# Feed-forward of a two-part float32 product: activations' hi and lo parts side by side as 512 moving columns

## The chip, the cores and the metric

The kernel runs on one core of one Trainium2 chip. The metric is device time in microseconds (us) of one execution; the median of three runs is given. TensorE (PE) multiplies matrices, with its weight loads shown apart (PEld), VectorE is called DVE, ScalarE ACT, GpSimd POOL, SyncE SP. The kernel's matmul results go to eight banks of PSUM, each of 128 partitions by 512 float32 numbers; everything else lies in SBUF.

## What is computed

256 tokens of 1024 numbers go through eight feed-forward stages and four mixers, in float32, one after another:

```python
def _swiglu(h, w_gate, w_up, w_down):
    return (jax.nn.silu(h @ w_gate) * (h @ w_up)) @ w_down

# first block, twice: feed-forward, mixer (rwkv, then mla), feed-forward, each behind an rms norm
x = x + 0.5 * _swiglu(_rmsnorm(x, g[0]), w_gate, w_up, w_down)
...
# second block, twice: feed-forward, mixer (nsa, then hgrn), feed-forward, each followed by a layer norm
x = _layer_norm(alpha * x + 0.5 * _swiglu_2(x, w_gate, w_up, w_down), gain, bias)
```

`w_gate` and `w_up` are 1024 x 2816, `w_down` is 2816 x 1024, and each stage has its own. The stages are FFN1, rwkv, FFN2, FFN3, mla, FFN4, FFN5, nsa, FFN6, FFN7, hgrn, FFN8. Only the feed-forward stages are changed.

## The kernel before

Float32 accuracy is had by two parts: a number is hi + lo, each in PE's float32r format, and a product is taken as ah bh + ah bl + al bh, three matmuls. `mm3` (L169 to L181) issues them: for each 128 rows of the contraction the two products with the stationary hi part, then those with the stationary lo part.

`weights` (L155) loads 1 MB of a weight matrix by a DMA of SP's queue (L165) into one of four staging tiles (`st0`, `st1`, and the stage's own `xst0`, `xst1`), and `hi_lo` (L149) splits it, half by half: ACT copies to hi (L152: `sp0h`, `sp1h`, `xsp0h`, `xsp1h`), DVE subtracts for lo (L153: `sp0l` and so on). There are four split tiles, too, used in turn.

The activations stand transposed, as `xTh` and `xTl`, each 128 x 8 x 256 (`new_xT`, L190; `transpose_split`, L196, writes them out of a bank, ACT the hi part, DVE the lo part).

A feed-forward stage (`_ffn`, L334) goes over the 2816 hidden channels in 11 units of 256. In the usual unit the weights are stationary and the 256 tokens stream. Its four blocks of 128 channels are gate 0, gate 1, up 0 and up 1; a block has a bank of its own and takes 24 matmuls of 256 columns. Behind them come, for each half of the channels, Silu on ACT (L346, `s`), the product with up on DVE (L351, `h`), its hi part by ACT (L402, `hTh`) and its lo part by DVE (L403, `hTl`). Then PE does the down product of the unit before: 24 matmuls in which 512 columns of the down weights stream, into four banks `acc` that collect over the whole stage. Four banks `rot` go round for everything else.

All stages but FFN1 start while the stage before is still finishing the second half of the tokens (`self.second`, called by `finish`). There the first two units go token block by token block: 128 tokens are stationary, and 256 columns of the weights stream. Their results `h` are transposed later (`late`). At a stage's end the last unit's down product has no work behind it: units 9 and 10 are multiplied token block by token block, and what follows on ACT and DVE is the split of the next stage's first weights.

A scheduler orders each engine's instructions by its own estimates; a queue's order is then fixed, and each engine works in order.

## Time and profile before

| what | value |
| --- | --- |
| three runs | 2179.0 to 2186.6 us, median 2181.73 us |
| profiled execution, span | 2183.2 us |
| PE busy | 2128.8 us, 98% |
| PE weight loads busy | 1955.2 us, 90% |
| DVE busy | 1253.8 us, 57% |
| ACT busy | 1003.9 us, 46% |
| eight feed-forward stages | about 190 us each (FFN2 390 to 580) |

Shares are of the span. Matmuls are pipelined: the duration that a row gives for one is longer than the distance from its start to the next one's, and it is that distance that counts. A row "x8" is eight instructions alike, and its time is that of all together. The profiled execution is one of its own, beside the three runs.

### The profile page before, as it was taken

Reading aid. Unit: us, or ns where it says so; the run is one execution under the profiler, and the core shown is the slowest. Engines: PE = TensorE matmul, PEld = TensorE weight load, DVE = VectorE, ACT = ScalarE, POOL = GpSimd, SP = SyncE. Lnnn points to the kernel's source line nnn. Section 1 sums busy time; section 2 is a strip of 40 time slices with the busy share of each in tenths; the row PEclk is TensorE's granted clock in tenths of the full one; section 3 lists DMA queues with packets and bytes.
Section 4 is the critical chain, followed back from the end, with each engine's and each line's share of the span. In section 5 each row is a group of like instructions: output and inputs, shape, how many; then the busy total and the mean of one; then the engine's idle time right before and its main releaser. Section 6 shows DMA issues by size and latency. Waiting matters only on the chain. (4 is left out here: it accounts for less than half of the span.)

```text
span 2183.2 us, 36275 instructions
## 1 busy us (share of the span) xinstructions
PE 2128.8 (98%) x15049; PEld 1955.2 (90%) x15049; DVE 1253.8 (57%) x2034; ACT 1003.9 (46%) x1750; POOL 183.8 (8%) x344
## 2 busy tenths in 40 slices
PE   8999999999999999999998999999999999999998
PEld 7998887999999977999897998689999999988997
DVE  5554765645555467645553566765565546766554
ACT  5444643544444455544442445544434444444442
POOL 2001050000100032000000010100000000241000
PEclk9999999999999999999999999999999999999999
DMA  9653433555556344755468563165546546326551
GB/s 302 207 180 99 141 104 119 203 187 180 176 196 205 121 135 150 239 175 192 145 212 171 168 205 116 39 205 182 192 155 225 187 155 199 130 78 232 187 185 54
DMA packets 271349, 367.63 MB, mean 168 GB/s; under 512 B 6865, under 2 KB 236853, under 8 KB 271184
## 3 DMA queue, kind: packets, MB, share of 16 engines
q1 hardware_dynamic: 263984, 348.48, 48.2%
q0 software_dynamic: 5088, 15.79, 3.3%
q8 instruction: 118, 1.93, 0.4%
q10 hardware_dynamic: 2112, 1.05, 0.2%
q14 instruction: 47, 0.39, 0.1%
HBM read 358.87 MB, written 6.42 MB: 167 GB/s over the span
## 5 line engine op out<-in xcount | busy, mean ns | idle before, releaser
L181 PE MATMUL rot<-xTh,sp0h 128*128 128x256 f32 (+1 forms) x976 | 243.3, 286 | 0.8 <-ACT xTh L205 0.8
L181 PE MATMUL rot<-xTl,sp0h 128*128 128x256 f32 (+1 forms) x976 | 240.3, 283 | 0.7 <-DVE xTl L206 0.7
L181 PE MATMUL rot<-xTh,sp1h 128*128 128x256 f32 x960 | 240.5, 287 | 0.0
L181 PE MATMUL rot<-xTl,sp1h 128*128 128x256 f32 x960 | 237.1, 283 | 0.0
L153 DVE TENSOR_TENSOR sp0l<-st,sp0h 128x1024 fp32r<-128x1024 f32 (+4 forms) x126 | 144.4, 1163 | 86.0 <-ACT sp0h L152 85.9
L181 PEld LDWEIGHTS rot<-xTh,sp0h 128*128 128x128 f32 (+1 forms) x976 | 186.7, 192 | 5.0 <-ACT xTh L205 1.7
L181 PEld LDWEIGHTS rot<-xTl,sp0h 128*128 128x128 f32 (+1 forms) x976 | 186.8, 192 | 2.7 <-DVE xTl L206 1.3
L181 PEld LDWEIGHTS rot<-xTh,sp1h 128*128 128x128 f32 x960 | 184.0, 192 | 3.1 <-issue 2.0
L181 PEld LDWEIGHTS rot<-xTl,sp1h 128*128 128x128 f32 x960 | 184.3, 192 | 0.7
L153 DVE TENSOR_TENSOR xsp0l<-xst,xsp0h 128x1024 fp32r<-128x1024 f32 (+4 forms) x106 | 116.8, 1128 | 103.8 <-ACT xsp0h L152 103.7
L351 DVE TENSOR_TENSOR h<-rot,s 128x256 f32<-128x256 f32 x176 | 74.3, 422 | 158.3 <-PE rot L181 147.1
L152 ACT ACTIVATE sp0h<-st 128x1024 fp32r<-128x1024 f32 (+4 forms) x126 | 122.0, 1003 | 83.2 <-issue 33.7
L153 DVE TENSOR_TENSOR xsp1l<-st,xsp1h 128x1024 fp32r<-128x1024 f32 x80 | 95.6, 1221 | 98.3 <-ACT xsp1h L152 98.3
L152 ACT ACTIVATE xsp0h<-xst 128x1024 fp32r<-128x1024 f32 (+4 forms) x106 | 99.5, 979 | 106.2 <-DMA xst<-in_ffn_w_gate_dram 65.4
L153 DVE TENSOR_TENSOR sp1l<-st,sp1h 128x1024 fp32r<-128x1024 f32 (+3 forms) x108 | 122.4, 1146 | 35.7 <-ACT sp1h L152 35.5
L181 PE MATMUL rot<-xTh,sp0l 128*128 128x256 f32 (+1 forms) x976 | 141.8, 282 | 0.0
L181 PE MATMUL rot<-xTh,sp1l 128*128 128x256 f32 x960 | 140.2, 283 | 0.0
L153 DVE TENSOR_TENSOR sp1l<-xst,sp1h 128x1024 fp32r<-128x1024 f32 x80 | 95.6, 1220 | 73.1 <-ACT sp1h L152 73.1
L152 ACT ACTIVATE xsp1h<-st 128x1024 fp32r<-128x1024 f32 x80 | 81.1, 1052 | 109.7 <-PE rot L181 39.8
L181 PEld LDWEIGHTS rot<-xTh,sp0l 128*128 128x128 f32 (+1 forms) x976 | 127.4, 191 | 0.2 <-issue 0.2
L181 PEld LDWEIGHTS rot<-xTh,sp1l 128*128 128x128 f32 x960 | 126.2, 192 | 0.0
L346 ACT ACTIVATE s<-rot 128x256 f32<-128x256 f32 x176 | 66.2, 376 | 130.1 <-PE rot L181 109.9
(573 smaller groups left out, 5360.4 us busy)
## 6 DMA issues: line engine op xcount, KB each, us to landing
st<-in_ffn_w_up_dram SPq DMA_DIRECT2D x47, 1024.0 KB, 5.3
st<-in_ffn_w_gate_dram SPq DMA_DIRECT2D x47, 1024.0 KB, 5.2
xst<-in_ffn_w_down_dram SPq DMA_DIRECT2D x47, 1024.0 KB, 5.1
xst<-in_ffn_w_up_dram SPq DMA_DIRECT2D x41, 1024.0 KB, 5.3
st<-in_ffn_w_down_dram SPq DMA_DIRECT2D x41, 1024.0 KB, 4.9
xst<-in_ffn_w_gate_dram SPq DMA_DIRECT2D x40, 1024.0 KB, 5.3
st<-in_even_w_in_dram SPq DMA_DIRECT2D x12, 1024.0 KB, 5.2
st<-in_hgrn_w_in_dram SPq DMA_DIRECT2D x8, 1024.0 KB, 5.6
```

The source lines that it names most:

```text
L152: self.nc.scalar.activation(hi[:, s], src[:, s], AF.Copy)
L153: self.nc.vector.tensor_sub(lo[:, s], src[:, s], hi[:, s].bitcast(F32))
L181: self.last_mm = nc.tensor.matmul(out, a, b, start=start and i == 0, stop=stop and i == n - 1).ins
L346: self.last_act = nc.scalar.activation(s, g, AF.Silu).ins
L351: self.last_mul = nc.vector.tensor_mul(h, u, s).ins
```

## The change

`xTh` and `xTl` become the two halves of one tile `xT`, 128 x 8 x 2 x 256, so that for each of the eight k blocks the 256 hi columns and the 256 lo columns stand side by side. In the usual unit, `mm_wide` replaces `mm3`: a stationary hi block of the weights is multiplied by all 512 columns at once, hi results in the lower half of the bank, lo results in the upper; the stationary lo block by the 256 hi columns, into the lower half. A block has 8 matmuls of 512 columns and 8 of 256. The halves are then added by `joined`: ACT copies the upper half to SBUF (`g`), DVE adds the lower to it. Silu and product take `g`.

The first two units become one of 512 channels: weights come as four k blocks by 512 columns, two loads for gate and two for up, and 512 columns of weights stream through the tokens, 24 matmuls of 512 per matrix and token block; Silu and product are 512 wide.

The core of the diff (the rest takes comments out):

```diff
     def new_xT(self, pool=None):
         pool = pool or self.keep
-        hi = pool.tile([P, KD, T], F32R, tag="xTh", name=self.n("xTh"))
-        lo = pool.tile([P, KD, T], F32R, tag="xTl", name=self.n("xTl"))
-        return hi, lo
+        both = pool.tile([P, KD, 2, T], F32R, tag="xT", name=self.n("xT"))
+        return both[:, :, 0, :], both[:, :, 1, :], both
+
+    def mm_wide(self, b, terms):
+        nc, n = self.nc, len(terms)
+        for i, (wh, _, _, both) in enumerate(terms):
+            nc.tensor.matmul(b, wh, both.rearrange("p a n -> p (a n)"), start=i == 0, stop=False, skip_group_check=True)
+        for i, (_, wl, xh, _) in enumerate(terms):
+            self.last_mm = nc.tensor.matmul(b[:, :T], wl, xh, start=False, stop=i == n - 1, skip_group_check=True).ins
...
+        def joined(b):
+            g = self.ff.tile([P, T], F32, tag="g", name=self.n("g"))
+            nc.scalar.activation(g, b[:, T:], AF.Copy)
+            nc.vector.tensor_add(g, b[:, :T], g)
+            return g
...
-            ws = [(unit(wg, u), unit(wu, u)) for u in range(2)]
+            ws = [[self.weights(w, k0, 4, 0, 2 * N) for k0 in (0, 4)] for w in (wg, wu)]
             for t in range(2):
...
-                for u in range(2):
-                    b = []
-                    for wh, wl in ws[u]:
-                        b.append(self.bank())
-                        self.mm3(b[-1][:, :N], [(xT[0][:, k, ts], xT[1][:, k, ts], wh[:, k, :], wl[:, k, :])
-                                                for k in range(KD)], True, True)
-                    if t and u == 0:
+                b = []
+                for halves in ws:
+                    b.append(self.bank())
+                    for j, (wh, wl) in enumerate(halves):
+                        self.mm3(b[-1], [(xT[0][:, 4 * j + k, ts], xT[1][:, 4 * j + k, ts], wh[:, k, :], wl[:, k, :])
+                                         for k in range(4)], j == 0, j == 1)
+                    if t and len(b) == 1:
...
-                    h = mul(act(b[0][:, :N]), b[1][:, :N])
-                    late.append((h, ys[u], t, 0, 2))
+                h = mul(act(b[0], 2 * N), b[1], 2 * N)
+                late += [(h[:, u * N:(u + 1) * N], ys[u], t, 0, 2) for u in range(2)]
...
-                    self.mm3(b[-1][:, :T], [(wh[:, k, s], wl[:, k, s], xT[0][:, k, :], xT[1][:, k, :])
-                                            for k in range(KD)], True, True)
+                    self.mm_wide(b[-1], [(wh[:, k, s], wl[:, k, s], xT[0][:, k, :], xT[2][:, k])
+                                         for k in range(KD)])
...
-                h = mul(act(b[i][:, :T]), b[2 + i][:, :T])
+                h = mul(act(joined(b[i])), joined(b[2 + i]))
```

The lines of `_ffn` get other numbers: in the changed kernel the copy is L365, the add L366, Silu L354, the product L359, hTh L417, hTl L418, `mm_wide` L200 and L202, the layer norm's last step L291, `transpose_split` L209 to L214.

The order on PE in the last unit of FFN2, the end of block gate 0 and the start of gate 1, before (`rot` are the banks, `xTh` and `xTl` the moving activations, `sp0h` and `sp0l` the gate weights):

```order
L181 MATMUL rot_5772<-xTh_4099,sp0h_5766 128x256
L181 MATMUL rot_5772<-xTl_4100,sp0h_5766 128x256
L181 MATMUL rot_5772<-xTh_4099,sp0l_5767 128x256 x8
L181 MATMUL rot_5797<-xTh_4099,sp0h_5766 128x256
L181 MATMUL rot_5797<-xTl_4100,sp0h_5766 128x256
```

The first three blocks of the same unit in the changed kernel (`sp0` gate, `sp1` up):

```order
L200 MATMUL rot_5280<-xT_3876,sp0h_5274 128x512 x8
L202 MATMUL rot_5280<-xT_3876,sp0l_5275 128x256 x8
L200 MATMUL rot_5297<-xT_3876,sp0h_5274 128x512 x8
L202 MATMUL rot_5297<-xT_3876,sp0l_5275 128x256 x8
L200 MATMUL rot_5322<-xT_3876,sp1h_5316 128x512 x8
L202 MATMUL rot_5322<-xT_3876,sp1l_5317 128x256 x8
```

Sixteen matmuls of 256 columns for the hi part, alternating, have become eight of 512; the eight for the lo part stand as before.

DVE behind the same unit, at the end of FFN2, before; `rot_5830` and `rot_5855` are the two up blocks, `sp0l` and `sp1l` the next stage's first weights:

```order
L351 TENSOR_TENSOR h_5884<-rot_5830,s_5882 128x256
L153 TENSOR_TENSOR sp0l_6008<-st_830_6005,sp0h_6007 128x1024
L403 TENSOR_TENSOR hTl_5881<-h_5884,hTh_5880 128x256
L153 TENSOR_TENSOR sp0l_6008<-st_830_6005,sp0h_6007 128x1024
L351 TENSOR_TENSOR h_5890<-rot_5855,s_5888 128x256
L153 TENSOR_TENSOR sp1l_6016<-st_833_6013,sp1h_6015 128x1024
L403 TENSOR_TENSOR hTl_5881<-h_5890,hTh_5880 128x256
L153 TENSOR_TENSOR sp1l_6016<-st_833_6013,sp1h_6015 128x1024
```

The same place in the changed kernel (`rot_5339` is the last up block, `g_5375` its sum):

```order
L359 TENSOR_TENSOR h_5366<-g_5363,s_5361 128x256
L153 TENSOR_TENSOR sp0l_5495<-st_897_5492,sp0h_5494 128x1024
L418 TENSOR_TENSOR hTl_5357<-h_5366,hTh_5356 128x256
L153 TENSOR_TENSOR sp0l_5495<-st_897_5492,sp0h_5494 128x1024
L366 TENSOR_TENSOR g_5375<-rot_5339,g_5375 128x256
L153 TENSOR_TENSOR sp1l_5503<-st_900_5500,sp1h_5502 128x1024
L359 TENSOR_TENSOR h_5378<-g_5375,s_5373 128x256
L153 TENSOR_TENSOR sp1l_5503<-st_900_5500,sp1h_5502 128x1024
L418 TENSOR_TENSOR hTl_5357<-h_5378,hTh_5356 128x256
```

The add of the last up block stands behind the split of the first weights, and one half of the next split stands between it and the product. On ACT the same place reads, before:

```order
L346 ACTIVATE s_5882<-rot_5772 128x256
L346 ACTIVATE s_5888<-rot_5797 128x256
L152 ACTIVATE sp0h_6007<-st_830_6005 128x1024
L402 ACTIVATE hTh_5880<-h_5884 128x256
L152 ACTIVATE sp0h_6007<-st_830_6005 128x1024
L152 ACTIVATE sp1h_6015<-st_833_6013 128x1024 x2
L402 ACTIVATE hTh_5880<-h_5890 128x256
```

and in the changed kernel:

```order
L365 ACTIVATE g_5358<-rot_5280 128x256
L354 ACTIVATE s_5361<-g_5358 128x256
L365 ACTIVATE g_5363<-rot_5322 128x256
L365 ACTIVATE g_5370<-rot_5297 128x256
L152 ACTIVATE sp0h_5494<-st_897_5492 128x1024
L354 ACTIVATE s_5373<-g_5370 128x256
L417 ACTIVATE hTh_5356<-h_5366 128x256
L152 ACTIVATE sp0h_5494<-st_897_5492 128x1024
L365 ACTIVATE g_5375<-rot_5339 128x256
L152 ACTIVATE sp1h_5502<-st_900_5500 128x1024 x2
L417 ACTIVATE hTh_5356<-h_5378 128x256
```

Four copies are added; the copy of the last up block stands behind both halves of the first split, and two halves of the second stand between it and the last `hTh`.

PE in the tail of FFN2, in the changed kernel, from the second half of unit 9's down product on (`hTh_5214` is unit 9's, `hTh_5356` unit 10's, `acc_3908` and `acc_3909` the first token block's banks, `acc_3910` the second's):

```order
L181 MATMUL acc_3909<-xsp0h_5384,hTh_5214 128x512
L181 MATMUL acc_3909<-xsp0l_5385,hTh_5214 128x512
L181 MATMUL acc_3909<-xsp0h_5384,hTl_5215 128x512 x2
L181 MATMUL acc_3908<-xsp1h_5392,hTh_5356 128x512
L181 MATMUL acc_3908<-xsp1l_5393,hTh_5356 128x512
L181 MATMUL acc_3909<-xsp1h_5392,hTh_5356 128x512
L181 MATMUL acc_3909<-xsp1l_5393,hTh_5356 128x512
L181 MATMUL acc_3910<-xsp0h_5384,hTh_5214 128x512
L181 MATMUL acc_3910<-xsp0l_5385,hTh_5214 128x512
L181 MATMUL acc_3908<-xsp1h_5392,hTh_5356 128x512
L181 MATMUL acc_3908<-xsp1l_5393,hTh_5356 128x512
L181 MATMUL acc_3908<-xsp1h_5392,hTl_5357 128x512
```

Before, the six matmuls of a bank stood together; now those that take the first half of unit 10's channels come first for both banks, then two of the second token block, and the second half of the channels behind them.

DVE at the start of FFN7, where the layer norm of the second token block (`x_82`) meets the split of the third weights, before:

```order
L278 BN_AGGR mv_16415<-bn_16412 128x2
L282 SCALAR_TENSOR_TENSOR x_82<-x_82,mv_16415,gain_16221 128x512 x2
L283 SCALAR_TENSOR_TENSOR x_82<-x_82,mv_16415,gain_16223 128x512 x2
L153 TENSOR_TENSOR xsp0l_16288<-xst_2202_16285,xsp0h_16287 128x1024 x2
L351 TENSOR_TENSOR h_16353<-rot_16326,s_16351 128x256
L153 TENSOR_TENSOR xsp1l_16296<-xst_2205_16293,xsp1h_16295 128x1024 x2
```

and in the changed kernel:

```order
L286 BN_AGGR mv_14688<-bn_14685 128x2
L290 SCALAR_TENSOR_TENSOR x_82<-x_82,mv_14688,gain_14549 128x512 x2
L291 SCALAR_TENSOR_TENSOR x_82<-x_82,mv_14688,gain_14551 128x512
L153 TENSOR_TENSOR xsp0l_14615<-xst_2373_14612,xsp0h_14614 128x1024 x2
L291 SCALAR_TENSOR_TENSOR x_82<-x_82,mv_14688,gain_14551 128x512
L214 TENSOR_TENSOR xT_14553<-rot_14696,xT_14553 128x4x128
L153 TENSOR_TENSOR xsp1l_14623<-xst_2376_14620,xsp1h_14622 128x1024 x2
L214 TENSOR_TENSOR xT_14553<-rot_14703,xT_14553 128x4x128
```

The split of the third weights (`xsp0l`) now stands ahead of the layer norm's last operation.

## Rows read from the trace of the kernel before

**Rows 1.** the page: span; busy time, share, instructions

```profile
span 2183.2 us, 36275 instructions
...
PE 2128.8 (98%) x15049; PEld 1955.2 (90%) x15049; DVE 1253.8 (57%) x2034; ACT 1003.9 (46%) x1750; POOL 183.8 (8%) x344
```

**Rows 2.** windows: length, busy (instructions) of PE PEld DVE ACT POOL, clock, DMA, GB/s

```profile
438.95:450.46 11.51, 11.51 (x97) 11.50 (x96) 5.57 (x6) 5.79 (x8) 0.00 (x0) 1.00 0.64 223
450.46:455.93 5.47, 5.47 (x26) 4.53 (x25) 3.03 (x4) 1.61 (x3) 0.00 (x0) 1.00 0.39 130
```

**Rows 3.** windows: the next whole unit, columns as in rows 2

```profile
455.93:472.91 16.98, 16.98 (x121) 16.02 (x120) 8.60 (x10) 7.17 (x10) 0.00 (x0) 1.00 0.57 183
```

**Rows 4.** windows: a unit of the seventh stage, columns as in rows 2

```profile
1743.29:1748.92 5.63, 5.63 (x27) 4.53 (x26) 3.03 (x4) 1.56 (x3) 0.00 (x0) 1.00 0.57 182
1748.92:1760.30 11.38, 11.38 (x97) 11.38 (x96) 5.58 (x6) 5.79 (x8) 0.00 (x0) 1.00 0.62 211
```

**Rows 5.** windows of PE alone: a first-unit token block, fourth and seventh stage

```profile
875.56:887.28 11.72, 11.72 (x96) 1.00 0.72 229
1631.98:1645.12 13.14, 12.36 (x99) 1.00 0.78 206
```

**Rows 6.** timeline, seventh stage: start, us, instruction, [idle before, releaser]

```profile
1636.28 1.42 DVE L283 SCALAR_TENSOR_TENSOR x<-x,mv,gain 128x512 f32<-128x512 f32 x2 [0.44 <-POOL mv L228]
1637.61 2.35 DVE L153 TENSOR_TENSOR xsp0l<-xst,xsp0h 128x1024 fp32r<-128x1024 f32 x2
...
1638.88 0.39 PE L181 MATMUL rot<-xsp0l,xTh 128*128 128x256 f32 x1 [0.78 <-DVE xsp0l L153]
```

**Rows 7.** source line L1618: durations ns min/median/max, starts

```profile
L1618 ACT ACTIVATE V<-rot x8: 383/384/387, 1826.6 to 1849.4; 128x256 f32<-128x256 f32 x8
```

**Rows 8.** lines by form: count | busy us, mean ns | idle, releasers

```profile
L153 DVE TENSOR_TENSOR sp0l<-st,sp0h 128x1024 fp32r<-128x1024 f32 x110 | 132.5, 1221 | 72.2 <-ACT sp0h L152 72.1
...
L152 ACT ACTIVATE sp0h<-st 128x1024 fp32r<-128x1024 f32 x110 | 112.1, 1052 | 77.7 <-issue 33.7 <-PE rot L181 17.7 <-PE acc L181 9.8
...
L351 DVE TENSOR_TENSOR h<-rot,s 128x256 f32<-128x256 f32 x176 | 74.3, 422 | 158.3 <-PE rot L181 147.1 <-PE rot L201 10.6
```

**Rows 9.** timeline, second stage: a weight split and its first use

```profile
496.54 2.35 DVE L153 TENSOR_TENSOR xsp1l<-st,xsp1h 128x1024 fp32r<-128x1024 f32 x2
...
506.88 0.28 PE L181 MATMUL rot<-xTh,xsp1h 128*128 128x256 f32 x1
```

**Rows 10.** timeline, end of the second stage

```profile
566.54 1.06 ACT L152 ACTIVATE sp0h<-st 128x1024 fp32r<-128x1024 f32 x1 [2.32 <-DMA st<-in_ffn_w_gate_dram]
...
569.33 0.40 PE L181 MATMUL acc<-xsp0h,hTh 128*128 128x512 f32 x1
...
570.70 0.42 ACT L402 ACTIVATE hTh<-h 128x256 fp32r<-128x256 f32 x1
...
572.53 0.39 PE L181 MATMUL acc<-xsp1h,hTh 128*128 128x512 f32 x1
```

**Rows 11.** DMA issues: KB each, us to landing

```profile
sk<-bs POOLq DMA_DIRECT2D x1, 3072.0 KB, 35.2
```

**Rows 12.** timeline, fifth stage, ACT

```profile
1192.05 1.06 ACT L152 ACTIVATE xsp0h<-xst 128x1024 fp32r<-128x1024 f32 x1 [27.23 <-DMA xst<-in_ffn_w_gate_dram]
```

**Rows 13.** waits of PE: us in total, times, longest

```profile
PE rot L181 <- ACT xsp1h L152: 10.0, 2, 9.3
```

**Rows 14.** timeline, first stage, PE

```profile
15.00 0.41 PE L181 MATMUL rot<-xTl,sp0h 128*128 128x256 f32 x1
15.21 0.41 PE L181 MATMUL rot<-xTh,sp0h 128*128 128x256 f32 x1
```

More of the change, by code (lines that the diff above doesn't have):

```diff
@@ L342, in hT, with act, mul @@
             return yh, yl
-        def act(g):
-            s = self.ff.tile([P, N], F32, tag="s", name=self.n("s"))
+        def act(g, n=N):
+            s = self.ff.tile([P, n], F32, tag="s", name=self.n("s"))
             self.last_act = nc.scalar.activation(s, g, AF.Silu).ins
             return s
-        def mul(s, u):
-            h = self.ff.tile([P, N], F32, tag="h", name=self.n("h"))
+        def mul(s, u, n=N):
+            h = self.ff.tile([P, n], F32, tag="h", name=self.n("h"))
             self.last_mul = nc.vector.tensor_mul(h, u, s).ins
             return h
+        def joined(b):
[3 more added lines that the diff above has]
+            return g
         ys, todo, first, late = [], [], 0, []
@@ L363, in _ffn @@
                     self.finish()
-                for u in range(2):
-                    b = []
-                    for wh, wl in ws[u]:
-                        b.append(self.bank())
-                        self.mm3(b[-1][:, :N], [(xT[0][:, k, ts], xT[1][:, k, ts], wh[:, k, :], wl[:, k, :])
-                                                for k in range(KD)], True, True)
-                    if t and u == 0:
+                b = []
[5 more added lines that the diff above has]
+                    if t and len(b) == 1:
                         while late:
                             self.transpose_split(*late.pop(0))
-                    h = mul(act(b[0][:, :N]), b[1][:, :N])
-                    late.append((h, ys[u], t, 0, 2))
-                todo = [(0, ys[0]), (1, ys[1])]
+                h = mul(act(b[0], 2 * N), b[1], 2 * N)
+                late += [(h[:, u * N:(u + 1) * N], ys[u], t, 0, 2) for u in range(2)]
+            todo = [(0, ys[0]), (1, ys[1])]
         NU = F // N
```

## The prediction

> **What bounds the kernel now.** I read the page first. The span is 2183.2 us and TensorE (PE) is busy in 98% of it [rows 1], so only what shortens PE's own stream, or what lets PE stand still, moves the end. Then I cut one steady feed-forward unit of the second stage (390 to 580 us) into its two parts by the windows view. The 96 matmuls of 256 columns take 11.51 us, the 24 of 512 columns 5.47 us, with PE busy throughout and the granted clock at 1.00 (its 2.4 GHz level) [rows 2]. That is 11.51 / 96 = 119.9 ns for a matmul of 256 columns and 5.47 / 24 = 227.9 ns for one of 512. Two of the small ones take 239.8 ns, one of the large ones 227.9: joining a pair is worth 11.9 ns where PE is never waiting. In the next whole unit of 16.98 us VectorE (DVE) is busy 8.60 us and ScalarE (ACT) 7.17 us [rows 3]: both have half their time free. Last I looked at the places where PE does wait: the starts of stages, their tails, and one stall.
>
> **Units behind the first ones.** A block (gate or up, 128 hidden channels) is now 8 matmuls of 512 and 8 of 256 in place of 24 of 256: 8 pairs joined, 32 in a unit, 0.38 us of 16.98. The first stage has 11 such units, the other seven 9 each: 74 units, 2368 pairs, 2368 x 11.9 ns = 28.2 us. How far can the price of a pair be off? The row of rows 2 is one unit. In a unit of the seventh stage, whose weights lie in other buffers, the 24 wide ones take 5.63 us (234.6 ns each) and the 96 small ones 11.38 us (118.5 ns) [rows 4]. With 234.6 against 119.9 a pair is worth 5.2 ns, with both prices of that unit 2.4 ns. The wide matmul that the change adds streams activations through stationary weights, where the timed wide one streams weights through stationary activations; no row shows that form. I take 11.9, since the first price is that of nearly all units and the form of the stationary part is the same 128x128, and keep 2.4 as the lower end.
>
> A rule of the Trainium skill speaks against most of this gain: "TensorE: Matmul & The Clock Gate", section "Back-to-back issue gap", gives an isolated matmul N / 2.4 ns and some 2.5 ns more, so that joining two saves 2.5 ns; 3040 pairs would then give 7.6 us. The rows above disagree with it for the steady units: 119.9 ns is 13.2 over 256 / 2.4 = 106.7.
>
> **First two units.** Per token block 96 matmuls of 256 become 48 of 512: 48 pairs, two token blocks, seven stages, 672 pairs, 8.0 us at 11.9 ns. One such block without a stall took 11.72 us for 96 matmuls, 122.1 ns each [rows 5]; at that price a pair is worth 16.3 ns and the sum 11.0. I take 8.0 and keep 11.0 as the upper end. The weights are the same bytes in pieces of 512 columns.
>
> In the seventh stage this part takes 13.14 us with PE busy for 12.36 [rows 5]: 0.78 us of idle lie in it. DVE does the last two layer-norm operations (1.42 us) ahead of the split of the third weights, and the split begins only at 1637.61, where PE needs it; PE's wait ends at 1638.88 [rows 6]. In the new order one of the two operations stands behind that split (the order of DVE above), so it can start 0.7 us sooner. The eighth stage has the same wait. I count 0.5 us for each, 1.0 (bounds 0 and 1.6).
>
> **What is added.** Per block one ACT copy of 256 columns out of a bank and one DVE add: 296 of each. An ACT copy of this form stands elsewhere in the trace at 384 ns [rows 7]; for the add I take the product of the same size, 422 ns [rows 8]. A unit gains 4 x 0.384 = 1.5 us on ACT (7.17 to 8.7) and 4 x 0.422 = 1.7 us on DVE (8.60 to 10.3), both below the new unit of 16.6 us. I cost them at nothing in the steady units. What hides them: a bank comes round again after three other blocks (2.8 us each) and a down product (5.5 us), 13.8 us, against a copy, an add and at most two splits of weights ahead of each; the weights that the splits make ready are done at 498.9, and PE takes them up at 506.88 [rows 9], 8 us of slack; the hidden channels are consumed a unit later. If that cover were gone, a unit would wait at least once for a copy and an add, 0.81 us, twice the 0.38 that it gains; nothing in the rows is that near.
>
> **Tails.** At the end of a stage the cover is short: the last unit's channels are consumed at once. In the second stage the last block ends and the down product begins at 569.33. ACT writes the last hTh from 570.70 on, done at 571.12, and PE takes it up at 572.53, 14 matmuls later: 1.4 us of slack [rows 10]. Now the chain behind the last block E is longer. One after the other come the ACT copy (0.38), the DVE add (0.42), half a weight split that stands next on DVE (1.22, [rows 8]), the product (0.42), and hTh on ACT (0.42), whose own queue has two halves of a split (2.1) in the meantime: 2.9 us. I allow 0.3 for the passes from engine to engine, and 0.5 to 1.2 for the half split that DVE is in when the copy is done: E + 3.7 to E + 4.4. In the new order of PE 18 matmuls stand ahead of the first use of that half (12 of unit 9, four with the other half of the channels, two of the next token block): 18 x 228 ns, E + 4.1. The lo part has another half split ahead of it and is due three matmuls later, so it is late by a little more. Each tail loses between nothing and 2 us (a whole split more ahead of the copy). I take 0.4, near the late end, in seven tails (behind the eighth stage no weights are split): -2.8 us.
>
> **Stall.** In the fifth stage a transfer of 3 MB that takes 35.2 us [rows 11] holds up the weights: ACT waits 27.23 us for a gate matrix, until 1192.05 [rows 12], and PE 9.3 us for a split of weights [rows 13]. The transfer is issued behind a unit's last activation, so it moves with the work, but what PE saves while it runs is waited for again: two units of 16.98 us, -0.8 us.
>
> **Cold clock.** At the start of the first stage, at the 1.2 GHz level, small matmuls follow one another in 0.21 us [rows 14], which is 256 / 1.2 GHz = 213 ns with nothing over, so a pair saves nothing there; those few pairs come to some 0.1 us and are left out.
>
> **Sum.** 28.2 + 8.0 + 1.0 - 2.8 - 0.8 = 33.6 us. From the profiled execution, 2183.2, this gives 2149.6. That execution lies 1.5 us above the median of the runs (2181.7), so the forecast is 2148.1. Bounds of the likeliest case: 3.0 more from the first units, 0.6 from the layer norms and 2.8 from tails without loss give 2141.7; tails of 2 us each cost 11.2 more, 2159.3.
>
> **Rivals.**
> Wide matmuls dearer: if activations as the moving part take 234.6 ns, a pair gives 5.2 ns, 15.8 us in all, 13.2 with the rest: 2168.5. For it: rows 4, and that no row has the form. Against: that price is tied to some buffers of some stages.
>
> Nothing saved: at 2.4 ns, 7.3 us in all, 4.7 with the rest, 2177.0. That is also about where the skill's rule (2.5 ns) would put it. Against: the unit of rows 2 is what most of the trace repeats.
>
> Slower, by the tails: ACT works in order, and the copy of the last block stands behind the split of the next stage's first weights, which waits for their transfer. In the second stage that landed at 566.54 [rows 10], 2.8 us ahead of E; the split, a Silu, hTh and the split's other half (2.9 us) fill that, so a transfer that is later by d makes hTh late by nearly d. Without tails the gain is 36.4; to be over 0.3% (6.5 us, about what a measurement can tell from no change) slower, each of seven tails must lose 6.1 us, so transfers must land some 6 us later. For it: the wait of 2.32 us on that transfer shows that it is not early, and ACT, more loaded, frees staging buffers later. Against: 6 us is a whole transfer's length. At the point of decision: 2188.
>
> **Chances.** Forecast 0.77, dearer wide matmuls 0.09, nothing saved 0.06, slower by the tails 0.08. Faster by over 0.3% 0.86, within 0.3% 0.06, slower 0.08. The range 2139 to 2166 holds the likeliest case with its bounds and part of the way to the dearer matmuls.
>
> **What would show it.** In the changed profile a steady unit should take 16.6 us, its four blocks 11.13 us: 32 matmuls of 512 at 228 ns and 32 of 256 at 120 ns. 234 ns there means the first rival. A first-unit token block should take 10.9 us and its transposes. PE's waits for hTh and hTl at stage ends should come to some 3 us in all; over 10 us would mean the tails. The copies and adds should show 384 and 422 ns, 296 each, and no PE wait for a bank (ACT or DVE at the added lines) in mid-stage. The prediction is wrong if the new form has a price of its own, or if PE waits inside units.

## The result, and the profile after

| runs | median us | lowest to highest |
| --- | --- | --- |
| before, 4 | 2180.78 | 2179.0 to 2186.6 |
| changed, 4 | 2155.79 | 2152.85 to 2159.59 |

The ratio is 0.9879 with a 95% interval of 0.9864 to 0.9894: the change gains 25.0 us by the medians, where 33.6 was forecast. The time lies in the range given (2139 to 2166), 7.8 us above the forecast of 2148. The two profiled executions differ by 2183.2 - 2157.5 = 25.7 us. (A span is about 2 us shorter than the time of the same execution: the changed kernel's 2157.5 belongs to the run of 2159.59. The prediction set 2183.2, a span, beside 2181.7, a time; its forecast, the median less 33.6, doesn't hang on that.)

The page of the changed kernel begins with the span and the busy time and instruction count of each engine:

```profile
span 2157.5 us, 30733 instructions
...
PE 2102.0 (97%) x12009; PEld 1796.4 (83%) x12009; DVE 1356.1 (63%) x2316; ACT 1103.6 (51%) x2032; POOL 186.7 (9%) x344
```

Beside [rows 1], PE has 15049 - 12009 = 3040 matmuls fewer, the number of pairs that was counted (2368 + 672). DVE and ACT are each 100 us busier and still far from full.

The windows view of the steady unit of the second stage that answers to [rows 2 and 3]; columns are length, busy time (instructions) of PE, PEld, DVE, ACT and POOL, granted clock, DMA share, GB/s:

```profile
438.98:450.12 11.14, 11.14 (x65) 9.82 (x64) 6.66 (x9) 6.77 (x11) 0.00 (x0) 1.00 0.84 282
450.12:455.59 5.47, 5.47 (x27) 4.51 (x25) 3.45 (x5) 2.05 (x4) 0.00 (x0) 1.00 0.43 143
455.59:472.20 16.61, 16.61 (x89) 14.34 (x88) 9.84 (x14) 8.48 (x14) 0.00 (x0) 1.00 0.63 194
```

The four blocks take 11.14 us in place of 11.51 (11.13 was forecast), a whole unit 16.61 in place of 16.98 (16.6 forecast). PE never waits in it; DVE is busy for 9.84 us and ACT for 8.48.

The added operations, in the view of lines by form (count, busy us and mean ns, then the engine's idle time before them):

```profile
L365 ACT ACTIVATE g<-rot 128x256 f32<-128x256 f32 x296 | 103.9, 377 | 167.2 <-PE rot L202 167.2
...
L366 DVE TENSOR_TENSOR g<-rot,g 128x256 f32<-128x256 f32 x296 | 117.7, 418 | 80.8 <-ACT g L365 80.6
```

That is 296 of each at 377 and 418 ns (384 and 422 forecast). Both engines wait for PE here, and PE's waits of the whole trace (us in total, times, longest) name neither line:

```profile
PE rot L200 <- ACT xsp1h L152: 10.9, 1, 10.9
PE rot L209 <- DVE xn L278: 9.3, 2, 8.3
PE rot L181 <- DVE sp0l L153: 2.5, 2, 1.4
...
PE rot L181 <- DVE xsp0l L153: 1.9, 4, 0.7
PE rot L200 <- DVE xT L214: 1.3, 1, 1.3
```

The first is the stall of the fifth stage, 10.9 us where it was 9.3 [rows 13]. The third and the last are new; both come from first matmuls that now take in more at once, and are read below.

Where did 7.9 us of the forecast go? I cut both profiled executions at the first matmul of each part:

| part of the span, us | before | changed | difference | forecast |
| --- | --- | --- | --- | --- |
| up to the first matmul | 13.46 | 14.52 | +1.1 | 0 |
| first units, seven stages | 180.9 | 172.2 | -8.7 | -9.0 |
| usual units, with the stall | 1265.8 | 1242.1 | -23.7 | -27.4 |
| tails, eight stages | 87.5 | 89.3 | +1.8 | +2.8 |
| mixers and the rest | 635.5 | 639.4 | +3.9 | 0 |
| sum | 2183.2 | 2157.5 | -25.7 | -33.6 |

(Rounded parts differ from the sum by 0.1.) The forecast's 27.4 is 28.2 less the 0.8 of the stall; its 9.0 is 8.0 for the pairs and 1.0 for the layer-norm waits. Three rows are off: usual units by 3.7 us, the start by 1.1, and the mixers, which the change doesn't touch, by 3.9. In the first units two misses of opposite sign cancel. Six stages gained 11.4 us together. FFN2, for which a gain was summed as well, lost 2.7 us (25.76 to 28.47). Its start in the changed kernel, PE's timeline (start, us, instruction, idle before and releaser):

```profile
388.01 0.50 PE L181 MATMUL rot<-sp0h,xT 128*128 128x512 f32 x1 [0.76 <-ACT xT L213]
...
389.89 0.50 PE L181 MATMUL rot<-sp0l,xT 128*128 128x512 f32 x1 [1.38 <-DVE sp0l L153]
...
392.22 0.73 PE L181 MATMUL rot<-sp0l,xT 128*128 128x512 f32 x1 [1.14 <-DVE sp0l L153]
```

and DVE's, which makes the lo parts of these weights:

```profile
385.75 2.35 DVE L153 TENSOR_TENSOR sp1l<-st,sp1h 128x1024 fp32r<-128x1024 f32 x2
...
388.62 1.21 DVE L153 TENSOR_TENSOR sp0l<-st,sp0h 128x1024 fp32r<-128x1024 f32 x1
389.75 1.28 DVE L214 TENSOR_TENSOR xT<-rot,xT 128x512 fp32r<-128x512 f32 x2
390.95 1.21 DVE L153 TENSOR_TENSOR sp0l<-st,sp0h 128x1024 fp32r<-128x1024 f32 x1
```

A 512-wide gate product needs both halves of the k blocks, `sp0` and `sp1`. `sp1` is ready when PE comes. `sp0` comes late: PE reads its buffer up to the end of the mixer ahead (ACT's copy to `sp0h` begins at 386.42), and on DVE the first half of `sp0l` stands behind `sp1l`, the second behind the activations' lo part (L214, 1.28 us). Before, the halves of `sp0l` came no sooner: in both kernels their splits begin 0.61 and 2.94 us behind the first matmul (before at 390.34). But there the up product from `sp1` ran meanwhile, and PE waited for them for 0.31 us. Now PE waits twice, and the granted clock falls behind the waits (windows of PE alone):

```profile
386.00:392.00 6.00, 2.94 (x15) 1.00 0.00 0
392.00:396.00 4.00, 3.78 (x10) 0.57 0.66 184
396.00:404.00 8.00, 8.00 (x38) 1.00 1.07 386
```

PE was busy for 2.94 of 6.00 us; in the next 4 us it had 0.57 of its 2.4 GHz, near the lower level of 1.2, then 1.00 again.

### The profile page after: what moved, and what is told of

Same layout as the page of the kernel before. It is cut to its first block, busy times and chain, and to the rows that moved or that the text cites. A ratio compares the mean times of both kernels' runs of the same rounds, so it can differ in the third digit from the quotient of the medians.

```text
span 2157.5 us, 30733 instructions
## 1 busy us (share of the span) xinstructions
PE 2102.0 (97%) x12009; PEld 1796.4 (83%) x12009; DVE 1356.1 (63%) x2316; ACT 1103.6 (51%) x2032; POOL 186.7 (9%) x344
## 5 line engine op out<-in xcount | busy, mean ns | idle before, releaser
L200 PE MATMUL rot<-xT,sp1h 128*128 128x512 f32 x784 | 196.7, 393 | 0.0
L200 PE MATMUL rot<-xT,sp0h 128*128 128x512 f32 x768 | 194.4, 395 | 1.3 <-DVE xT L214 1.3
L365 ACT ACTIVATE g<-rot 128x256 f32<-128x256 f32 x296 | 103.9, 377 | 167.2 <-PE rot L202 167.2
L153 DVE TENSOR_TENSOR xsp0l<-xst,xsp0h 128x1024 fp32r<-128x1024 f32 (+4 forms) x106 | 116.9, 1127 | 89.3 <-ACT xsp0h L152 89.2
L366 DVE TENSOR_TENSOR g<-rot,g 128x256 f32<-128x256 f32 x296 | 117.7, 418 | 80.8 <-ACT g L365 80.6
L200 PEld LDWEIGHTS rot<-xT,sp0h 128*128 128x128 f32 x768 | 141.4, 190 | 28.8 <-DVE xT L214 1.7
L200 PEld LDWEIGHTS rot<-xT,sp1h 128*128 128x128 f32 x784 | 142.0, 189 | 26.4
L417 ACT ACTIVATE hTh<-h 128x256 fp32r<-128x256 f32 x148 | 61.7, 417 | 123.9 <-DVE h L359 123.9
L202 PEld LDWEIGHTS rot<-xT,sp1l 128*128 128x128 f32 x784 | 106.9, 190 | 7.7
L200 PE MATMUL rot<-xT,xsp1h 128*128 128x512 f32 x400 | 102.2, 398 | 10.9 <-ACT xsp1h L152 10.9
L202 PEld LDWEIGHTS rot<-xT,sp0l 128*128 128x128 f32 x768 | 105.5, 191 | 7.9
L202 PE MATMUL rot<-xT,sp1l 128*128 128x256 f32 x784 | 109.2, 282 | 0.0
L202 PE MATMUL rot<-xT,sp0l 128*128 128x256 f32 x768 | 107.6, 283 | 0.0
L200 PE MATMUL rot<-xT,xsp0h 128*128 128x512 f32 x416 | 104.6, 393 | 0.0
```

The lines of the kernel that those rows point to most:

```text
L153: self.nc.vector.tensor_sub(lo[:, s], src[:, s], hi[:, s].bitcast(F32))
L200: nc.tensor.matmul(b, wh, both.rearrange("p a n -> p (a n)"), start=i == 0, stop=False, skip_group_check=True)
L202: self.last_mm = nc.tensor.matmul(b[:, :T], wl, xh, start=False, stop=i == n - 1, skip_group_check=True).ins
L365: nc.scalar.activation(g, b[:, T:], AF.Copy)
L366: nc.vector.tensor_add(g, b[:, :T], g)
L417: nc.scalar.activation(y[0][:, i, :], h, AF.Copy)
```

## The experiments

All were timed beside the kernel before; "parts" are those of the table above.

**The changed kernel once more (e0).** Is the mixers' +3.9 us the change's?

> The changed kernel again, unaltered, for the spread of its own time and for one question: in its first profile the mla mixer took 3.9 us longer than before, at a granted clock of 0.68 to 0.96 where before had 1.00. Theory A (the drop of the clock in mla is chance, the change did not cause it): median 2153 to 2157, and a profile whose mla stretch (end of the third stage to start of the fourth) is again about 104.9 us, or at least runs of two kinds some 4 us apart. Theory B (the change brings it): mla again takes some 108.7 us.

2153.05 us (2151.71 to 2159.15), ratio 0.9872 [0.9853, 0.9891]. In its profile the feed-forward parts, with the start, come to 1519.3 us (1518.1 in the first one), the rest to 637.8. Mla took 106.3 us, which is the number of neither theory. The mixers rwkv and mla as windows of PE alone, in the profile of the kernel before:

```profile
204.40:390.30 185.90, 183.20 (x1497) 0.97 0.34 110
770.70:875.50 104.80, 98.01 (x515) 1.00 0.42 138
```

In that of the changed kernel:

```profile
202.10:388.00 185.90, 183.31 (x1497) 0.97 0.35 110
763.10:871.80 108.70, 101.84 (x515) 0.95 0.40 134
```

In that of e0:

```profile
202.40:383.40 181.00, 178.62 (x1497) 1.00 0.36 113
759.40:865.70 106.30, 99.48 (x515) 0.98 0.42 137
```

And of the kernel before in a second profile (e11, below):

```profile
203.40:390.90 187.50, 184.85 (x1497) 0.96 0.34 109
771.10:877.20 106.10, 99.20 (x516) 0.98 0.42 135
```

The length goes with the granted clock: rwkv takes 181 us at 1.00 and 186 to 187.5 at 0.97 and 0.96; mla 104.8 at 1.00 and 108.7 at 0.95. One program shows several of these clocks.

**Usual units alone (e1).** The first two units are as before the change; the usual ones are wide.

```diff
-            ws = [[self.weights(w, k0, 4, 0, 2 * N) for k0 in (0, 4)] for w in (wg, wu)]
+            ws = [(unit(wg, u), unit(wu, u)) for u in range(2)]
```

> Only the usual units are wide; the first two units of the stages go as before, 256 columns of weights at a time. Theory A (each matmul has a part of its time that does not grow with its columns, some 11 ns of it saved per joined pair; the gain adds up from the two parts of the change): the steady part gains its 23.7 us, the first units stand as before, 2163 to 2167. Rival (the two parts hide or spoil one another): under 2160 or over 2170.

2160.18 us (2158.95 to 2160.99), 0.9898 [0.9881, 0.9915]. Usual units 1241.9 us, as in the changed kernel; first units 181.5, as before, FFN2's 25.77. The whole time is some 3 us under the bounds given, 0.2 us from the rival's: the mixers and the rest took 630.9 us in this profile, the least of all. In the parts nothing spoils the other. Most of the gain is here.

**First units alone (e2).** The usual units multiply as before.

```diff
-                    self.mm_wide(b[-1], [(wh[:, k, s], wl[:, k, s], xT[0][:, k, :], xT[2][:, k])
+                    self.mm3(b[-1][:, :T], [(wh[:, k, s], wl[:, k, s], xT[0][:, k, :], xT[1][:, k, :])
```

> Only the first two units are 512 wide; the usual units are multiplied as before, without joins. Theory A: the first units gain 8 to 11 us and everything else stays, 2170 to 2173; the first product of the second stage again waits for the split of its first weights (some 2.5 us) and its first units take about 28.5 us in place of 25.8. Rival (that wait comes from the wide units' loading of ACT and DVE): the second stage's first units take about 24 us here.

2178.38 us over 12 runs (2174.39 to 2181.98), 0.9982 [0.9971, 0.9994]: missed. In the parts it holds: first units 171.8 us (-9.1), with FFN2's at 27.37, so its wait is there without any wide unit ahead. But the mixers and the rest took 639.9 us in this profile (rwkv 187.62), 4.4 more than in the first profile of before. It isn't this profile alone: the 12 runs have a mean granted clock of 0.989, the 23 of the kernel before beside them 0.991. A slow stretch in FFN2 like that of the changed kernel (4.00 us at 0.57) would explain 0.001 of it; what lowers the rest stays open. The lowest of the 12 runs lies 4.3 us under the lowest of those 23.

**Each wide matmul as two of 256 (e3).** Order, copies and adds are those of the change; only the 512 columns are cut.

```diff
-            nc.tensor.matmul(b, wh, both.rearrange("p a n -> p (a n)"), start=i == 0, stop=False, skip_group_check=True)
+            for j in range(2):
+                nc.tensor.matmul(b[:, j * T:(j + 1) * T], wh, both[:, j, :], start=i == 0 and j == 0, stop=False, skip_group_check=True)
```

> The changed kernel, but each wide matmul of the usual units is issued as two of 256 columns, the hi part into the lower half of the bank, then the lo part into the upper: same products, same joins, same order on ACT and DVE, only the number of matmuls and weight loads is that of before. Theory A (fixed part per matmul): the steady part returns to its 1266 us and the joins cost nothing, so 23 to 26 us more than the changed kernel, 2178 to 2182. Rival (the gain comes from the new order of the products or the layout of the activations, not from the number of matmuls): 2156. Second rival (the joins cost something in the steady part that the wide matmuls more than pay for): over 2185.

2183.58 us (2179.84 to 2191.06), 1.0014 [1.0002, 1.0026]. That is 1.6 us over the bounds given. The usual units take 1266.3 us, before 1265.8. The second stage's usual units before (windows of PE alone):

```profile
416.10:569.33 153.23, 153.23 (x1086) 1.00 0.53 178
```

In the changed kernel:

```profile
416.48:566.41 149.93, 149.93 (x797) 1.00 0.56 183
```

And in e3:

```profile
414.44:567.67 153.23, 153.23 (x1086) 1.00 0.55 179
```

With the copies and adds and the old number of matmuls the stage takes what it took before. So the gain in the units comes from the number of matmuls, each with its weight load, and the joins cost nothing there. Matmul and load aren't told apart by this. But loads that set the pace of the narrow matmuls (PEld is busy for 11.50 of 11.51 us in [rows 2]) would leave the wide ones at 512 / 2.4 = 213 ns, at one column a clock; these take 229.2 from start to start in the changed kernel, so both widths carry a fixed part. The first units gain as in the change (172.9); the tails take 93.2 us, 4 more than in the changed kernel; why stays open.

**FFN2's first product from its ready half (e4).**

```diff
+                    order = (1, 0) if self.stage == 2 and t == 0 and len(b) == 1 else (0, 1)
+                    for m, j in enumerate(order):
+                        wh, wl = halves[j]
-                                         for k in range(4)], j == 0, j == 1)
+                                         for k in range(4)], m == 0, m == 1)
```

> The changed kernel, but in the second stage the first product begins with the half of the contraction whose weights are split first (buffer sp1), and takes the other half (sp0) behind it. Theory A (that stage's start is 2.7 to 3.5 us longer than before, not 1.7 shorter, because one product now needs both halves and the order of its matmuls puts the one split last first; PE's two waits of 2.5 us together are followed by some 4 us at the 1.2 GHz level): its first units go from 28.5 to 29.3 down to about 24 us, 4 to 5 us off the whole, 2148 to 2151. Rival (the second half comes no earlier, so the wait only moves): under 1 us. Side question: if mla again shows its granted clock at 1.00, its drop in the profiles so far was chance.

2149.84 us (2149.21 to 2156.56), 0.9856 [0.9832, 0.988], as expected. PE's timeline at the start of FFN2:

```profile
382.65 0.50 PE L181 MATMUL rot<-sp1h,xT 128*128 128x512 f32 x1 [1.25 <-ACT xT L213]
...
386.27 0.39 PE L181 MATMUL rot<-sp0h,xT 128*128 128x512 f32 x1
```

The window of FFN2's first units, PE alone:

```profile
382.65:406.78 24.13, 23.65 (x109) 1.00 0.70 241
```

PE waits for the activations (1.25 us; 0.76 in the changed kernel), but comes to `sp0h` without a wait; the clock stays at 1.00, and the part takes 24.13 us where the changed kernel's two profiles have 28.47 and 29.25.

**No copies and adds (e5).** The upper half of the bank, the lo activations' product, is left out of the result.

```diff
-                h = mul(act(joined(b[i])), joined(b[2 + i]))
+                h = mul(act(b[i][:, :T]), b[2 + i][:, :T])
```

> The changed kernel without the copies and adds: the upper half of each bank, the product with the activations' lo part, is left out of the result; Silu and product read the lower half. Theory A (copies and adds lie beside other work but at the tails, where they cost 1.8 us in all): 1 to 3 us less than the changed kernel, 2150 to 2153, the steady part as it was (1242 us). Rival (their load on ACT and DVE holds up weight splits or banks in the steady part, and that is where the gain fell short of the forecast): 4 us less or more, and a shorter steady part.

2157.44 us (2155.78 to 2161.79), 0.9884 [0.9865, 0.9902]: missed as a whole time. In the parts the tails are back at 87.5 us and the usual units at 1241.0, 1.1 less than in the changed kernel; the mixers and the rest took 639.6, and the four runs have the lowest mean clock of all (0.987). So the joins cost the tails 1.8 us and the units at most 1.1.

**FFN1's first block narrow as well (e6).** e4, and the very first gate block in matmuls of 256 columns that begin with the hi part, without a join.

```diff
+                    if first == u == i == 0 and w is wg:
+                        for j, (p, x) in enumerate(((wh, 0), (wl, 0), (wh, 1))):
+                            for k in range(KD):
+                                nc.tensor.matmul(b[-1][:, :T], p[:, k, s], xT[x][:, k, :],
+                                                 start=j == k == 0, stop=j == 2 and k == KD - 1)
+                        continue
```

> The second stage's start as in the run with the swapped halves; and the very first block of the first stage is multiplied as before, in matmuls of 256 columns, hi activations first, without a join, because a wide matmul needs the lo part too before it can start and saves nothing at the 1.2 GHz level. Theory A (the first wide matmul starts 1.06 us later than the first small one did, for want of the lo part): another 0.5 to 1.2 us, 2147.5 to 2150. Rival (the start is held by the transposes and their evictions, whichever matmul follows): no difference to the run with the swapped halves.

2147.05 us (2145.56 to 2147.6), 0.9832 [0.9817, 0.9847], a little under the bounds given. In the changed kernel the start reads, in PE's timeline,

```profile
14.52 0.80 PE L200 MATMUL rot<-xT,sp0h 128*128 128x512 f32 x1 [1.28 <-DVE xT L214]
```

and here that wait is 0.24 us. But the transposes ahead began later in this execution, and the first matmul stands at 14.30: this profile doesn't show 1.1 us won. Others do: with this start it stands at 13.32 to 13.60 in e7 to e10, and at 13.66 in e3, whose first matmul needs only the hi part; in the five profiles that begin with a wide matmul (changed, e0, e1, e4, e5) it stands at 14.36 to 14.71.

**The last up block of a stage narrow (e7).** e6, and block up 1 of the last unit by `mm3`, without a join.

```diff
+                    if u == NU - 1 and i == 1 and w is wu:
+                        self.mm3(b[-1][:, :T], [(wh[:, k, s], wl[:, k, s], xT[0][:, k, :], xT[1][:, k, :])
+                                                for k in range(KD)], True, True)
+                        continue
```

> As the run before, and the last block of each stage (up 1 of the last unit) is multiplied in matmuls of 256 columns as before, without copy and add, so that nothing is added to the chain at the tail. Theory A (the tails lose 1.8 us to that copy and add): the tails return to 87.5 us, eight blocks give back 8 x 8 x 11.9 ns = 0.8 us, 1 us less in all, 2146.5 to 2149. Rival (the tails are late through the other copies or the order of the splits): tails stay at 89 us and the time rises by 0.8.

2144.92 us (2143.2 to 2148.66), 0.9826 [0.9808, 0.9843], 1.6 us under the bounds given. Tails 87.5 us, as before the change; the first matmul is at 13.60.

**An unused tile of 32 bytes (e8).** What is still missing are the usual units of FFN1, FFN5 and FFN7. There a wide matmul takes 231.3 to 231.7 ns from start to start, in the other five stages 229.2; narrow ones there 119.1. In the first three the built program has the moving and the stationary operands begin 32 bytes apart, counted modulo 64, for the weights in `xsp`. e8 is e7 with a tile ahead of the stage's own, which shifts its buffers by 32 bytes:

```diff
+            if getattr(self, "stage", 0) + 1 in (1, 5, 7):
+                self.ff.tile([P, 8], F32, tag="pad", name=self.n("pad"), bufs=1)
```

> The run with the tail's last block as before, and a tile of 32 bytes per partition, never used, ahead of the stage's own tiles in stages one, five and seven. In those three stages the tiles of the stage (hidden channels, two of the four weight buffers) begin at a multiple of 64 bytes, while activations and the other two weight buffers begin 32 bytes off one; in the other five stages all begin 32 off. Theory C (the price of a matmul depends on whether its operands begin alike within 64 bytes; that is why wide matmuls cost 231.6 ns in stage seven against 229.2 in stage eight): stage seven's steady part falls from 151.0 to 149.9 us and those of one and five by as much, 3 to 3.5 us off the whole, 2141 to 2143. Rival (the price comes from something else in these stages, their own loads beside the work): no change.

2144.49 us (2142.9 to 2147.79), 0.9827 [0.9809, 0.9845]: not told from e7 by its time, and 1.5 us over the bounds given. Usual units of FFN1 in e7 (windows of PE alone):

```profile
13.60:189.49 175.89, 175.89 (x938) 1.00 0.64 207
```

And in e8:

```profile
13.41:186.79 173.38, 173.14 (x938) 1.00 0.65 210
```

FFN1 gains 2.5 us with the same matmuls at the same clock: those from `xsp` go from 233.3 to 229 ns. (With the same tile it takes 174.11 in e9, without it 175.11 in e10.) FFN7 gains only 0.4 of the 1.1 expected (151.12 to 150.72; 233.9 to 232.4 ns), though in e8's built program its operands begin alike modulo 64 too. FFN5 gains nothing as a whole (164.64 to 164.85): its matmuls from `xsp` fall as in FFN1 (233.7 to 229.6 ns), but its stall lasts 12.2 us in place of 10.0.

**The tile in the other five stages (e10).** The same with `in (2, 3, 4, 6, 8)`.

> The other way round: the 32 bytes are put ahead of the tiles of stages two, three, four, six and eight, so that all eight stages mix the two beginnings. Theory C: each of the five steady parts rises by some 1.1 us, from 149.9 to 151.0, 5.5 us in all, 2149 to 2152. Rival: no change, 2145.

2151.23 us (2148.67 to 2154.49), 0.9861 [0.9839, 0.9882], as expected. The second stage's usual units in e7:

```profile
406.10:556.12 150.02, 150.02 (x805) 1.00 0.55 182
```

And here:

```profile
405.46:556.19 150.73, 150.73 (x805) 1.00 0.55 182
```

0.70 us worse (1.1 expected), and so in each of the five: wide matmuls from `xsp` go from 229.3 to 232.8 ns. The five give 3.5 us and the first units 1.3, of the 6.3 by which the median is above e7's; that the whole time lies within the bounds is in part luck.

**Tiles under the mixers' buffers too (e9).** e8, with such a tile in the pools of four mixers as well: `pc.tile([P, 8], F32, name="pad")` in three, `p.tile([P, 8], F32, name="padm")` in mla.

> The same shift by 32 bytes, but made under the tiles of three mixers too, and a pad in the fourth, so that activations and weight buffers of the mixers begin alike as well. Theory C: the three stages as in the run before, and the mixers' 512-column products, 234 ns now for those from the common weight buffers, fall to 227 to 228: some 200 of them, another 1 to 1.5 us, 2139.5 to 2142. Rival: as above, 2145.

2143.97 us (2140.52 to 2147.62), 0.9823 [0.9802, 0.9843]. That is 2 us over the bounds given, the lowest median of all, and not to be told from e7 or e8. The trace shows the mixers' 512-column matmuls faster in part: from e8 to e9 their mean goes from 232.0 to 228.3 ns in nsa, from 233.4 to 232.0 in rwkv, from 231.5 to 230.5 in mla and from 230.5 to 229.7 in hgrn, some 0.6 us together where 1 to 1.5 were expected. The three stand at 0.9823 to 0.9827 of the kernel before, the changed kernel at 0.9879: the small edits of e4, e6 and e7 are worth about another half per cent.

**The kernel before once more (e11).** The rival for the mixers was that something in the changed kernel (other addresses, say) lowers their clock.

> The kernel before, once more, for a second profile of its mla mixer. All profiles with 512-wide first units show a drop of the granted clock there (105.8 to 108.7 us from the third stage's end to the fourth's start), the two without do not (104.9). Theory D (the drop belongs to those kernels): 104.9 us and a clock of 1.00 again. Rival (chance from run to run): a drop here too, or a time other than 104.9.

2184.3 us over 8 runs (2178.83 to 2185.98), 1.0006 [0.9993, 1.0019]. Its profile shows the drop: rwkv 187.56 us, mla 105.97, mixers and rest 638.5. e10, a changed kernel, has mla at 104.87 and a clock of 1.00. So a lowered clock in the mixers comes in kernels of both kinds, and the rival falls as it was put. That the change has no part in how often it comes isn't shown: the runs of the five programs with FFN2's waits (changed, e0, e2, e3, e5) have mean clocks of 0.987 to 0.990, those of all others 0.990 to 0.993.

The feed-forward parts scatter too. With the start they take 1545.7 us in this profile, 1547.7 in the first one of before: FFN1's usual units 178.91 for 180.00, FFN5's first units 26.37 for 27.88, since two waits of 0.7 us for weight splits are missing. By the means of two profiles each the change gains 28.0 us there, of the 33.6 forecast.

## Why the prediction was right, and where it was off

**The mechanism was right.** Joining two matmuls saves a fixed part of about 12 ns, where PE never waits. e3 is the test: everything else kept, the matmuls cut again, and the stage's 153.23 us are back. The Trainium skill's rule for an isolated matmul that was weighed in the prediction ("TensorE: Matmul & The Clock Gate", section "Back-to-back issue gap") would give 2368 x 2.5 ns = 5.9 us for the usual units, an estimate from its figure; 23.7 were measured, so the trace disagrees with it here.

**Units: the pair was mis-sized.** The forecast priced a pair at 11.9 ns everywhere (-28.2), and said that the dearer price of [rows 4] belongs to some buffers of some stages. It does, and the changed kernel has it as well. Five stages (FFN2, 3, 4, 6 and 8) went from 153.23 to 149.93 or 149.94, -3.30 where 9 x 0.38 = 3.43 had been summed: a pair is worth 11.5 ns. FFN1 went from 180.00 to 176.36 (-3.6, 4.2 summed; -2.6 from the second profile of before), FFN7 from 153.03 to 151.04 (-2.0, 3.4 summed); e8 shows up to 2.5 us of FFN1's time and 0.4 of FFN7's to be the operands' addresses. What keeps FFN7 0.7 us above the other stages in e8 stays open. FFN5 gained 1.66 of 3.43: its stall grew by 1.6 us, where 0.8 had been taken. ACT's wait there still hangs on the transfer, now until 1180.23, and a copy stands between the halves of the next split:

```profile
1180.23 1.06 ACT L152 ACTIVATE xsp0h<-xst 128x1024 fp32r<-128x1024 f32 x1 [26.32 <-DMA xst<-in_ffn_w_gate_dram]
1181.19 0.37 ACT L365 ACTIVATE g<-rot 128x256 f32<-128x256 f32 x1
```

The copy isn't the cause, for before a Silu of the same length stood in its place:

```profile
1193.02 0.36 ACT L346 ACTIVATE s<-rot 128x256 f32<-128x256 f32 x1
```

From the landing to PE's next matmul it is 3.27 us in both (1192.05 to 1195.32, 1180.23 to 1183.50), and in e5, which has no copies, too. What differs is how long PE stands there before the landing. The stall lasts 9.3 and 9.6 us in the two profiles of before and 9.8 to 12.4 in those with wide units, so the 0.8 us that its growth is too large by lie within its scatter.

**First units: one step failed.** "The weights are the same bytes in pieces of 512 columns" is true of the bytes, and the step drawn from it, that nothing but matmuls changes, failed in FFN2. A wide product needs both k halves before it can end, and it began with the one that is split last. FFN2 lost 2.7 us where FFN3 and FFN4 gained 1.7 each: a miss of 4.4, of which the two waits are 2.2 (1.38 + 1.14, less the 0.31 of before) and the slow stretch 1.7 (4.00 us at 0.57 of the clock). e2 has the wait without wide units, e4 takes it away by the order of two halves. The other six stages gained 11.4 us where 7.9 were summed (6 x 96 x 11.9 ns and 1.0 for the layer norms), but 1.5 of them are the two waits in FFN5 that the second profile of before doesn't have. So it is luck that the row's -8.7 stands so near the -9.0 summed; from the second profile it is -7.2. In FFN3 and FFN4 the gain comes to 1.7 / 96 = 17.7 ns a pair, over the 16.3 that was kept as an upper end.

**Layer norms: right in kind.** PE's wait in FFN7 fell from 0.78 [rows 6] to 0.41 us:

```profile
1621.77 0.51 PE L181 MATMUL rot<-xsp0l,xT 128*128 128x512 f32 x1 [0.41 <-DVE xsp0l L153]
```

and in FFN8 from 0.77 to 0.47: 0.7 us together, for 1.0.

**Tails: right in kind, 1.8 us for 2.8.** Behind the last block of FFN2 the down product begins at E = 566.41 and takes up the second half of the channels at 570.55 (PE's timeline):

```profile
566.41 0.40 PE L181 MATMUL acc<-xsp0h,hTh 128*128 128x512 f32 x1
...
570.55 0.50 PE L181 MATMUL acc<-xsp1h,hTh 128*128 128x512 f32 x1
```

In between, ACT does this:

```profile
566.88 0.38 ACT L365 ACTIVATE g<-rot 128x256 f32<-128x256 f32 x1
...
570.08 0.42 ACT L417 ACTIVATE hTh<-h 128x256 fp32r<-128x256 f32 x1 [0.93 <-DVE h L359]
```

and DVE this:

```profile
568.16 0.41 DVE L366 TENSOR_TENSOR g<-rot,g 128x256 f32<-128x256 f32 x1
568.50 1.21 DVE L153 TENSOR_TENSOR sp1l<-st,sp1h 128x1024 fp32r<-128x1024 f32 x1
569.63 0.42 DVE L359 TENSOR_TENSOR h<-g,s 128x256 f32<-128x256 f32 x1
```

It is the chain as predicted: copy, add, half a split between the add and the product, `hTh`. It ends at 570.50, E + 4.1, where E + 3.7 to 4.4 was given and PE wants it at E + 4.1, so PE is held up by little more than 0.1 us. Seven tails take 11.07 to 11.36 us where they took 10.91 to 10.93; FFN8's is as it was. The rival of tails that eat the gain falls: e5 and e7, which take the join away there, give back the 1.8.

**The start: not costed.** FFN1's first matmul now needs the lo activations too and waits 1.28 us for them. Its stretch is 1.1 us longer. e6 takes the wait away, and the profiles of e7 to e10 show about that time won.

**Mixers: +3.9 us that lie within the scatter.** e0, e10 and e11 show that they scatter by the granted clock, in kernels of both kinds: the mixers and the rest took 630.9 to 639.9 us over 14 profiles, and the first of before (635.5) and of the changed kernel (639.4) lie within that. Of the 8 us by which the profiled pair falls short, 3.9 are this, 3.7 the usual units, 1.1 the start, 0.3 the first units, and the tails give 1.0 back. Whether the change makes the lower clock more frequent stays open (e2, e11). Medians hold some of it too: e0's is 2.7 us under that of the same kernel's first runs, and those of the kernel before went from 2180.70 to 2184.72 with the chip and the runs.

## What to carry to other kernels

Where PE never waits, count the matmuls beside the columns: joining two that share their stationary operand gave 11.5 ns each here, and the copy and add that it needs are free as long as their engines have slack. A joined product can't begin before all its inputs are there: look for the places where PE stands right behind the last of them (starts and tails), and order the halves by when they are ready, or leave one block narrow. When runs of one program scatter by a few us, judge an edit of that size by the profile's own parts, not by whole times.

## What the runs showed of the hardware

A matmul's time hangs on where its operands begin. With 32 bytes of shift in front of a stage's buffers, wide matmuls from `xsp` went from 229.3 to 232.8 ns (e10) or from 233.3 to 229 (e8), and the 512-column down products of `sp1` from 227.8 to about 233 (e10). Whether operands begin alike modulo 64 isn't the whole rule: in FFN7 of e8 they do, and its wide matmuls from `xsp` still take 232.4 ns.

The granted clock falls for a while behind a wait of PE, and not alike from one execution to the next of one program. In rwkv two executions of the changed kernel part at one place (windows of PE alone). The first profile:

```profile
295.00:300.00 5.00, 4.39 (x20) 1.00 0.65 217
300.00:305.00 5.00, 5.00 (x16) 0.52 0.29 98
305.00:310.00 5.00, 5.00 (x36) 0.50 0.29 69
```

And e0:

```profile
295.00:300.00 5.00, 4.59 (x21) 1.00 0.65 190
300.00:305.00 5.00, 5.00 (x47) 1.00 0.56 177
305.00:310.00 5.00, 5.00 (x77) 1.00 0.11 16
```

PE waited for 0.61 of 5 us in the one and for 0.41 in the other; only the one then had 10 us at the lower level of 1.2 GHz, which are the 5 us by which its rwkv is longer. Mla in the changed kernel had 0.95 and 0.98 as a mean.
